# Two-layer hybrid encoder: the MLP's first product with tokens in the rows, its convolution from moved copies, products down in 16, 16 and 12 row tiles

## The chip, the core and the metric

The kernel runs on one core of one Trainium2 chip. The time is device microseconds of one execution; a median is taken over several runs. A profile is one further execution taken by the hardware profiler. Engines: TensorE (PE, its weight loads PEld), VectorE (DVE), ScalarE (ACT), GpSimd (POOL) and SyncE (SP), which only issues DMAs. ScalarE and GpSimd can issue DMAs too, each on a queue of its own. Every engine takes its list of instructions in order and waits at the head of it; 16 DMA engines carry what the queues issue.

## The reference

Two layers on x (256 tokens by 2048), float32. Each layer has a token mixer (attention and a Fourier branch), a cross-attention into 256 memory tokens, and a gated MLP. Every part has an RMS norm before and after it. The change touches the MLP alone:

```python
def conv_ffn(h, w_up, conv_w, conv_b, w_down):
    u = h @ w_up                                  # (256, 2048) @ (2048, 11264)
    up = jnp.pad(u, ((0, 0), (1, 1), (0, 0)))
    u = up[:, :-2] * conv_w[0] + up[:, 1:-1] * conv_w[1] + up[:, 2:] * conv_w[2] + conv_b
    gate, val = u[..., :D_FF], u[..., D_FF:]
    return (jax.nn.gelu(gate, approximate=True) * val) @ w_down   # D_FF = 5632
```

The convolution runs over neighbouring tokens, with three taps and a bias of its own for each of the 11264 channels.

## The kernel before, in words

All products are made of three fp32r products: the operand and the weights are each split in a rounded part (`hi`) and a rest (`lo`), and hi*hi, hi*lo and lo*hi are summed. The activations' parts lie in SBUF (`A_ff`, `G`). Weights stream from HBM: `load` (L110) fetches 128 by 1024 numbers (512 KB, 4 KB in each of 128 partitions) on SP's queue into one of four buffers `w32`; `Unit.split` (L124) makes `whi` with a cast on ScalarE (L133) and `wlo` with a subtraction on VectorE (L134), four buffers each. A unit is two such loads. A load waits for the `wlo` that frees its buffer, a cast for the matmuls that free its `whi`.

**First product, before.** It is channel-major: `ws_chunk` (L163) takes 128 output channels and all 256 tokens. For each of the 16 row tiles, `block` (L148) issues two matmuls, with weights as the stationary operand: `whi` against the 512 columns of both parts of the tokens (L151), `wlo` against the 256 columns of the high part (L152). Channels stand in partitions, tokens along the free dimension. `merge` (L220) adds the two halves of the bank; `conv` (L1189) multiplies by the norm's factor for each token, then uses the taps as one scalar per partition: one activation with scale and bias (L1192) for the middle tap and the bias, and two operations on 255 columns (L1195, L1199) that read the neighbour tokens at an offset of one column. Then come Gelu (L1223), the product of gate and value (L1224), and the split into `G` (L228, L229). This is done 44 times a layer, for a gate chunk and its value chunk. The first 512 columns (`w_up_ko`) are an exception: they are made token-major within the sub-layer's boundary (`Columns`, L305) and turned by eight transposes (L1233).

**Product down, before.** `G` is made in four quarters of 11 row tiles. After each quarter `products` (L371) multiplies it with `w_dn` for four groups of 512 output columns and adds to `y`. `mm_rows` (L296) has the tokens as the stationary operand: for each row tile and each of two token blocks three matmuls of 512 columns (L301 to L303).

**The order of the work.** The Tile scheduler orders each engine's list from the program; the boundaries between sub-layers are ordered by hand. `projected` (L611) and `stream` (L639), which the token mixer uses already, prepare the next unit's weights, then multiply the current one, with a callback between row tiles.

Of the kernel before, what the change touches and what calls it, by code (L numbers as in the profile page):

```python
# [9 lines left out]
F32 = mybir.dt.float32  # L10
# [16 lines left out]
NQ = 4  # L27
QK = DFF // P // NQ
# [8 lines left out]
O_BG, O_CW0, O_CW1, O_CW2, O_CB, NPAR = 112, 144, 232, 320, 408, 496  # L37
# [7 lines left out]
def encoder(ctx: ExitStack, tc: tile.TileContext, t, out):  # L45
# [325 lines left out]
    def products(src, S, nk, begin, finish, last, ahead=(), made=None, mid=None):  # L371

        late = []
        for n in range(4):
            begin(n)
            pss = [psum(f"y{j}") for j in range(2)]
# [5 lines left out]
            for k0 in range(0, nk, 4):  # L385
                m = min(4, nk - k0)
                w = made or unit(src[n][:, k0 * 512 : (k0 + m) * 512], m * 512)
                made = None
                if k0 == 0 and n in ahead:
                    ahead[n]()  # L390
                for k in range(k0, k0 + m):
                    if k >= split_at:
                        late.append((n, pss, k, w, (k - k0) * 512))
                        continue
                    for j in range(2):
                        mm_rows(pss[j], S, k, j, w, (k - k0) * 512, k == 0, k == nk - 1)
            if split_at == nk:
                for j in range(2):
                    finish(j, n, pss[j])
            yield n  # L400
        for j in range(2):
            for i, (n, pss, k, w, col) in enumerate(late):
                mm_rows(pss[j], S, k, j, w, col, k == 0, k == nk - 1)
                if k == nk - 1:
                    finish(j, n, pss[j])
                if j and i + 1 == (mid or len(late) // 2):
                    yield 5
            yield 4 + 2 * j
# [304 lines left out]
    for l in range(L):  # L713
# [448 lines left out]
        cols = Columns(t["w_up_ko"][l], A)  # L1162

        def ahead_apart(y, cols, tags):
# [12 lines left out]
            return {1: lambda: prepare(0), 2: lambda: prepare(1), 3: lambda: sqrt_ahead(y.ss[:, 0, 0:1])}  # L1177

        steps = products(t["w_xo"][l], OX, 4, y.gain, taken, (2,), ahead_apart(y, cols, "B"), w_first)
        for n in range(4):  # L1180
            next(steps)
        ss = boundary(y, steps, par[:, O_FFNPRE : O_FFNPRE + KT], A, cols)
        ut = tmp2("ut"), tmp2("ut")
        ut = [u.rearrange("p a n -> p (a n)") for u in ut]
        for j in range(2):
            nc.scalar.copy(ut[j], cols.ps[j])


        def conv(u, c, name):  # L1189
            nc.vector.tensor_mul(u, u, pre.b)  # L1190
            r = tmp1(name)
            nc.scalar.activation(  # L1192
                r, u, AF.Identity, scale=par[:, O_CW1 + c : O_CW1 + c + 1], bias=par[:, O_CB + c : O_CB + c + 1]
            )
            nc.vector.scalar_tensor_tensor(  # L1195
                out=r[:, 1:T], in0=u[:, 0 : T - 1], scalar=par[:, O_CW0 + c : O_CW0 + c + 1], in1=r[:, 1:T],
                op0=ALU.mult, op1=ALU.add,
            )
            nc.vector.scalar_tensor_tensor(  # L1199
                out=r[:, 0 : T - 1], in0=u[:, 1:T], scalar=par[:, O_CW2 + c : O_CW2 + c + 1], in1=r[:, 0 : T - 1],  # L1200
                op0=ALU.mult, op1=ALU.add,
            )
            return r

        NC = DFF // P
        G = [None] * NQ

        def up(c):

            qt, i = divmod(c, QK)  # L1210
            if i == 0:
                G[qt] = Rows("G") if qt % 2 == 0 else big.tile([P, QK, 2, T], F32R, tag="B", name="G")
            r = []
            for b in range(2):
                if c < 2:
                    u = tmp1("u")
                    nc.scalar.copy(u, firsts[c][:, b])
                else:
                    u = tmp1("u")
# [3 lines left out]
            nc.scalar.activation(r[0], r[0], AF.Gelu_apprx_tanh)  # L1223
            nc.vector.tensor_mul(r[0], r[0], r[1])  # L1224
            split(r[0], G[qt][:, i])

        pre = Pre()
        pre.of_squares(ss)
        third = [ws_chunk(t["w_up"][l, 0], A, KT, name="up")]
        firsts = [ps_sc.tile([P, 2, T], F32, tag="sc", name="ut") for _ in range(2)]  # L1230
        for i in range(4):
            for j in range(2):
                nc.tensor.transpose(  # L1233
                    firsts[i // 2][:, i % 2, j * P : (j + 1) * P], ut[j][:, i * P : (i + 1) * P], ident
                )
        pre.everywhere()
        third.append(ws_chunk(t["w_up"][l, 1], A, KT, name="up"))
        AHEAD = 1
        done = 0
        y = None  # L1240
        for qt in range(NQ):
            until = min(NC, (qt + 1) * QK + (AHEAD if qt + 1 < NQ else 0))
            for c in range(done, until):
                up(c)
            done = until
            if qt == 0:
                y = Out(t["gpost"][l, 2])
            more = qt == NQ - 1 and l + 1 < L

            def first_or_more(j, n, ps, qt=qt):  # L1250
                if qt == 0:
                    nc.scalar.copy(y.at(j, n), ps)
                elif qt < NQ - 1:
                    nc.vector.tensor_add(y.at(j, n), y.at(j, n), ps)
                else:
                    y.take(j, n, ps, True)

            if more:
                A = operand("A_mix")
                cols = Columns(t["w_vu"][l + 1, 0], A)  # L1260

            if more:
                before_last = ahead_apart(y, cols, "CD")
            else:
                before_last = {3: lambda y=y: sqrt_ahead(y.ss[:, 0, 0:1])}

            end = qt == NQ - 1
            steps = products(
                t["w_dn"][l, qt], G[qt], QK, y.gain if end else lambda n: None, first_or_more, 4 if end else QK,
                before_last if end else (), mid=5 if end else None,  # L1270
            )
            for n in range(4):
                next(steps)
            if qt < NQ - 1:
                run(steps)
# [90 lines left out]
def _layout(i):  # L1366
    NC = DFF // P
# [9 lines left out]
    for l in range(L):  # L1377
# [7 lines left out]
        for j, o in enumerate((O_CW0, O_CW1, O_CW2)):  # L1385
            par[l, :, o : o + 2 * NC] = _cols(i["conv_w"][l, j])
# [42 lines left out]
```

## Time and profile before

| | |
|---|---|
| median of 3 runs | 2911.51 us (2911.35 to 2911.95) |
| the profiled execution | 2912.27 us, span 2910.5 us |
| TensorE busy | 2897.6 us of the span |
| VectorE, ScalarE busy | 2053.4 us (71%), 1583.6 us (54%) |
| moved by DMA | 563.09 MB, mean 193 GB/s |
| granted TensorE clock | 0.999 |
| layer 0's MLP between its boundaries | from 744 to 1451 us of the span |
| layer 1's | from 2193.6 to 2896.9 us |

Busy time is the union of an engine's instructions; a matmul's end is modelled, so a busy TensorE says that it had work, not that it ran at its peak. In a group of instructions stand the line, the engine, what is written and read, shapes, the count, then busy time, the mean of one, the idle time just before them and what ended it.

### The profile page before, as it was taken

The page shows a single profiled execution, that of the slowest core. Times are in us where ns is not written, and L with a number is a line of the kernel's source. Part 1 is how long each engine was busy: PE and PEld are TensorE (multiplying, and loading weights), DVE is VectorE, ACT ScalarE, POOL GpSimd, SP SyncE. Part 2 cuts the span into 40 slices and gives each one's busy share as a digit, 9 for nine tenths or more (in the row PEclk, how much of TensorE's full clock was granted, in tenths as well). Part 3 has the DMA queues.
Part 4 walks back from the last instruction along what each step waited for, and adds up shares of the span by engine and source line. Part 5 has one row for each costly group of instructions (what it writes and reads, how often), then busy time and mean ns, then how long its engine had stood idle before and what let it go on. Part 6 is the DMA issues. An engine that isn't in the chain of part 4 may idle for free.

```text
span 2910.5 us, 39133 instructions
## 1 busy us (share of the span) xinstructions
PE 2897.6 (100%) x14476; PEld 2443.7 (84%) x14476; DVE 2053.4 (71%) x2930; ACT 1583.6 (54%) x2479; POOL 34.9 (1%) x60
## 2 busy tenths in 40 slices
PE   9999999999999999999999999999999999999998
PEld 7888888888888888888878888888888888888887
DVE  6668767666875867767776587776678768677676
ACT  6556455555655545545555564445566555455454
POOL 0000000000000000000000000000000000000000
PEclk9999999999999999999999999999999999999999
DMA  8644776765666566565655456677556666666655
GB/s 290 188 148 159 232 235 224 226 187 160 196 184 195 187 188 191 180 200 184 212 174 182 145 163 222 222 236 215 181 159 202 187 193 186 188 190 186 195 185 163
DMA packets 161775, 563.09 MB, mean 193 GB/s; under 512 B 18480, under 2 KB 19504, under 8 KB 161584
## 3 DMA queue, kind: packets, MB, share of 16 engines
q1 hardware_dynamic: 156816, 545.53, 59.5%
q0 software_dynamic: 4480, 14.68, 1.8%
q8 instruction: 113, 1.85, 0.3%
q14 instruction: 78, 0.64, 0.1%
q10 hardware_dynamic: 288, 0.39, 0.0%
HBM read 556.34 MB, written 4.19 MB: 193 GB/s over the span
## 4 chain that ended last, share of the span: by engine, by line
PE 97%; DVE 1%; ACT 1%; DMA 0%; issue 0%; DVEq 0%; ACTq 0%
PE up L151 22%; PE up L152 11%; PE y L302 8%; PE y L303 8%; PE y L301 8%; PE g L301 4%; PE g L303 4%; PE g L302 4%; PE qk L302 3%; PE qk L303 3%; PE qk L301 2%; PE a L301 2%; PE a L303 2%; PE a L302 2%; PE as L302 2%; PE as L301 2%
## 5 line engine op out<-in xcount | busy, mean ns | idle before, releaser
L134 DVE TENSOR_TENSOR wlo<-w,whi 128x1024 fp32r<-128x1024 f32 (+1 forms) x981 | 1179.9, 1205 | 656.4 <-ACT whi L133 649.4
L133 ACT CAST whi<-w 128x1024 fp32r<-128x1024 f32 (+1 forms) x981 | 1015.6, 1037 | 955.6 <-PE y L303 295.4
L151 PE MATMUL up<-A_ff,whi 128*128 128x512 f32 x2688 | 946.3, 397 | 0.0
L152 PE MATMUL up<-A_ff,wlo 128*128 128x256 f32 x2688 | 755.0, 281 | 0.0
L151 PEld LDWEIGHTS up<-A_ff,whi 128*128 128x128 f32 x2688 | 504.9, 188 | 121.9
L152 PEld LDWEIGHTS up<-A_ff,wlo 128*128 128x128 f32 x2688 | 509.0, 189 | 0.4
L301 PE MATMUL y<-whi,G 128*128 128x512 f32 x704 | 274.3, 390 | 0.0
L302 PE MATMUL y<-wlo,G 128*128 128x512 f32 x704 | 274.2, 389 | 0.0
L303 PE MATMUL y<-whi,G 128*128 128x512 f32 x704 | 274.2, 389 | 0.0
L301 PE MATMUL g<-whi,A_mix 128*128 128x512 f32 x512 | 202.3, 395 | 0.0
L302 PE MATMUL g<-wlo,A_mix 128*128 128x512 f32 x512 | 200.8, 392 | 0.0
L303 PE MATMUL g<-whi,A_mix 128*128 128x512 f32 x512 | 200.3, 391 | 0.0
L303 PEld LDWEIGHTS y<-whi,G 128*128 128x128 f32 x704 | 132.2, 188 | 27.5
L301 PEld LDWEIGHTS y<-whi,G 128*128 128x128 f32 x704 | 132.2, 188 | 27.4
L302 PEld LDWEIGHTS y<-wlo,G 128*128 128x128 f32 x704 | 132.2, 188 | 27.2
L303 PE MATMUL qk<-whi,A_mix 128*128 128x512 f32 x320 | 125.6, 392 | 0.0
L302 PE MATMUL qk<-wlo,A_mix 128*128 128x512 f32 x320 | 125.4, 392 | 0.0
L301 PE MATMUL qk<-whi,A_mix 128*128 128x512 f32 x320 | 124.9, 390 | 0.0
L223 ACT COPY t<-up 128x256 f32<-128x256 f32 x168 | 61.7, 367 | 102.8 <-DVE G L229 84.7
L303 PEld LDWEIGHTS g<-whi,A_mix 128*128 128x128 f32 x512 | 96.3, 188 | 19.1
L301 PEld LDWEIGHTS g<-whi,A_mix 128*128 128x128 f32 x512 | 96.3, 188 | 18.4
L302 PEld LDWEIGHTS g<-wlo,A_mix 128*128 128x128 f32 x512 | 96.4, 188 | 17.9
(264 smaller groups left out, 4076.7 us busy)
## 6 DMA issues: line engine op xcount, KB each, us to landing
w<-in_w_up SPq DMA_DIRECT2D x336, 512.0 KB, 4.5
w<-in_w_dn SPq DMA_DIRECT2D x160, 512.0 KB, 4.0
w<-in_w_g SPq DMA_DIRECT2D x128, 512.0 KB, 4.3
w<-in_w_qk SPq DMA_DIRECT2D x80, 512.0 KB, 4.5
w<-in_w_ao SPq DMA_DIRECT2D x64, 512.0 KB, 5.0
w<-in_w_mo SPq DMA_DIRECT2D x64, 512.0 KB, 4.3
w<-in_w_vu SPq DMA_DIRECT2D x47, 512.0 KB, 4.5
w<-in_w_fo SPq DMA_DIRECT2D x32, 512.0 KB, 4.1
```

Source lines behind the costliest of these rows:

```text
L133: nc.scalar.copy(hi[:, :m], w[:, :m])
L134: nc.vector.tensor_sub(lo[:, :m], w[:, :m], hi[:, :m].bitcast(F32))
L151: nc.tensor.matmul(ps, hi, a, start=first, stop=False, skip_group_check=True)
L152: nc.tensor.matmul(ps[:, :T], lo, a[:, 0:T], start=False, stop=last, skip_group_check=True)
L223: nc.scalar.copy(b, ps[:, T : 2 * T])
L301: nc.tensor.matmul(ps, ah, hi, start=first, stop=False)
L302: nc.tensor.matmul(ps, ah, lo, start=False, stop=False)
L303: nc.tensor.matmul(ps, al, hi, start=False, stop=last)
```

## The change

The first product is made token-major throughout. 11264 channels are 22 halves of 512: for column block b (0 to 10) the gate half and the value half. `projected` runs `mm_rows` over the 16 row tiles of a half, for two token blocks (`uv`, "gate" or "val": 128 partitions by 2 token blocks by 512 channels). `finish` evicts both with the norm's factor as scale. Tokens now stand in partitions, so a neighbour token is a neighbour partition. Two copies of the half are made by DMA on ScalarE's queue: `left` (L1240), moved up by one partition, and `right` (L1241), moved down by one; L1242 and L1243 copy the one row each that crosses from one token block to the other. The taps are fetched for each half with `partition_broadcast`, as 128 equal rows of 4 by 512 numbers (1 MB, `cv`, L1226, on SP's queue). VectorE multiplies left, right and own by their taps and sums (L1246, L1250, L1259), six operations on 1024 elements a partition. These are put into a list `due`, and `beside` issues them 7 to 12 row-tile steps after the half was finished. Gelu is one activation of 1024 elements. The gated result is turned by eight transposes a block into `G` (L1272, L1273, 13 and 14 steps after). Products down are made in 16, 16 and 12 row tiles, the first two in the same stream, after the gate halves of blocks 4 and 8; the last by `products`, which takes the first 8 row tiles of two column groups first. Parameters for taps and bias leave `par`; the weights' layout in HBM follows.

```diff
+        def half(i):
+            b, w = divmod(i, 2)
...
+            def finish(j, ps, to):
+                u = places["val" if w else "gate"]
+                nc.scalar.activation(u[:, j], ps, AF.Copy, scale=pre.t[:, j : j + 1])
+                if not j:
+                    return
+                left, right = places["left"], places["right"]
+                nc.scalar.dma_start(left[1:P], u[0 : P - 1])
+                nc.scalar.dma_start(right[0 : P - 1], u[1:P])
+                nc.scalar.dma_start(left[0:1, 1], u[P - 1 : P, 0])
+                nc.scalar.dma_start(right[P - 1 : P, 0], u[0:1, 1])
+
+                def times(v, k):
+                    nc.vector.tensor_mul(v, v, to[:, k : k + 1].to_broadcast([P, 2, 512]))
+
+                def own():
+                    times(u, 1)
+                    nc.vector.tensor_add(u, u, to[:, 3:4].to_broadcast([P, 2, 512]))
...
+                due.extend([(7, lambda: times(left, 0)), (8, lambda: times(right, 2)), (9, own)])
+                due.extend([(n, lambda v=v: nc.vector.tensor_add(u, u, v)) for n, v in ((10, left), (11, right))])
+                due.append((12, activate))
+                if w:
+                    due.extend([(13, lambda: turn(0)), (14, lambda: turn(1))])
+
+            def turn(j):
...
+                for m in range(4):
+                    nc.tensor.transpose(pt[:, m], places["val"][:, j, m * P : (m + 1) * P], ident)
+                hi, lo = [G[q][:, 4 * k : 4 * k + 4, part, j * P : (j + 1) * P] for part in range(2)]
+                nc.scalar.copy(hi, pt)
+                nc.vector.tensor_sub(lo, pt, hi.bitcast(F32))
...
+        def taps(i):
...
+            nc.sync.dma_start(to, t["conv"][l, :, h * 512 : (h + 1) * 512].partition_broadcast(P))
...
+        def up(i):
+            b, w = divmod(i, 2)
+            return projected(t["w_up"][l, b + w * NB], A, "up", half(i), lambda: taps(i))
...
+        for i in range(1, 2 * NB):
+            items += up(i)
+            b = i // 2
+            if i % 2 == 0 and b % DN == 0:
+                q = b // DN - 1
+                for n in range(4):
+                    src = down(q, n)
+                    items += projected([src[:, u * UW : (u + 1) * UW] for u in range(4)], Down(q), "y", sum_down(q, n))
...
-        def conv(u, c, name):
-            nc.vector.tensor_mul(u, u, pre.b)
-            r = tmp1(name)
-            nc.scalar.activation(
-                r, u, AF.Identity, scale=par[:, O_CW1 + c : O_CW1 + c + 1], bias=par[:, O_CB + c : O_CB + c + 1]
-            )
...
-                    ps = third[b] if c == 2 else ws_chunk(t["w_up"][l, 2 * (c - 2) + b], A, KT, name="up")
-                    merge(ps, u)
-                r.append(conv(u, b * NC + c, "cv"))
```

**VectorE, within the first product.** Before, a piece of layer 0 (`t_104` holds the chunk's 256 columns, `w_` numbers are weight buffers):

```order
L134 TENSOR_TENSOR wlo<-w_6935,whi 128x1024 [waits DMAHW7_49,PE_49,Activation_49]
L229 TENSOR_TENSOR G<-t_104,G 128x256 [waits Activation_49]
L224 TENSOR_TENSOR t_104<-up,t_104 128x256 [waits Activation_49]
L1190 TENSOR_TENSOR t_104<-t_104,rb 128x256 [waits DVE_49]
L134 TENSOR_TENSOR wlo<-w_6984,whi 128x1024 [waits DMAHW0_49,PE_49,Activation_49]
L1195 SCALAR_TENSOR_TENSOR t_104<-t_104,par_98 128x255 [waits Activation_49]
L1199 SCALAR_TENSOR_TENSOR t_104<-t_104,par_98 128x255 [waits DVE_49]
```

Now, after a gate half of layer 0 was finished (`uv` holds gate, val, left and right, `cv` the taps; `DMAHW` are the DMAs' semaphores; L135 is what L134 was, and w_8801 and w_8803 are the first unit of the next half, w_8839 and w_8841 the second, w_8877 and w_8879 the third):

```order
L135 TENSOR_TENSOR wlo<-w_8801,whi 128x1024 [waits DMAHW4_49,Activation_49]
L1246 TENSOR_TENSOR uv<-uv,cv 128x1024 [waits DMAHW3_49,DMAHW2_49]
L135 TENSOR_TENSOR wlo<-w_8803,whi 128x1024 [waits DMAHW5_49,PE_49,Activation_49]
L135 TENSOR_TENSOR wlo<-w_8839,whi 128x1024 [waits DMAHW7_49,Activation_49]
L135 TENSOR_TENSOR wlo<-w_8841,whi 128x1024 [waits DMAHW0_49,DVE_49,Activation_49]
L1246 TENSOR_TENSOR uv<-uv,cv 128x1024 [waits DMAHW5_49,DMAHW4_49,DVE_49]
L135 TENSOR_TENSOR wlo<-w_8877,whi 128x1024 [waits DMAHW1_49,Activation_49]
L135 TENSOR_TENSOR wlo<-w_8879,whi 128x1024 [waits DMAHW6_49,Activation_49]
L1246 TENSOR_TENSOR uv<-uv,cv 128x1024
L1250 TENSOR_TENSOR uv<-uv,cv 128x1024 [waits DVE_49]
L135 TENSOR_TENSOR wlo<-w_8919,whi 128x1024 [waits DMAHW7_49,Activation_49]
L1259 TENSOR_TENSOR uv<-uv 128x1024 [waits DVE_49]
```

Before, nothing on VectorE in this stretch but `wlo` waits for a DMA. Now the first L1246 (left) stands between the two `wlo` of one unit and waits for copies, and the second (right) ahead of the third unit's `wlo`.

**ScalarE, where a half is finished.** Before, a piece of layer 0's MLP:

```order
L228 CAST G<-t_104 128x256 [waits DVE_49]
L133 CAST whi<-w_7575 128x1024 [waits DMAHW0_49,PE_49]
L133 CAST whi<-w_7577 128x1024 [waits DMAHW1_49,PE_49,Activation_49]
L133 CAST whi<-w_7611 128x1024 [waits DMAHW2_49,PE_49,Activation_49]
L1252 COPY y<-y_7467 128x512 [waits PE_49]
```

Now, where the gate half of the rows above is finished (L1236 is the eviction):

```order
L1236 ACTIVATE uv<-up_8653,rstd_t 128x512 [waits PE_49]
L1236 ACTIVATE uv<-up_8654,rstd_t 128x512 [waits PE_49]
L1242 DMA uv<-uv 1x16x32 [waits Activation_49]
L1240 DMA uv<-uv 127x1024 [waits Activation_49]
L1241 DMA uv<-uv 127x1024
L1243 DMA uv<-uv 1x16x32 [waits DMAHW5_49]
L134 CAST whi<-w_8803 128x1024
L134 CAST whi<-w_8839 128x1024 [waits DMAHW7_49,PE_49]
```

And where a later value half is finished:

```order
L1236 ACTIVATE uv<-up_9147,rstd_t 128x512 [waits DVE_49]
L1236 ACTIVATE uv<-up_9148,rstd_t 128x512
L1272 CAST G<-gt 128x4x128 [waits PE_49] x2
L1240 DMA uv<-uv 127x1024 [waits DMAHW5_49,Activation_49]
L1241 DMA uv<-uv 127x1024 [waits DMAHW6_49]
L1242 DMA uv<-uv 1x16x32
L1243 DMA uv<-uv 1x16x32 [waits DMAHW7_49,DMAHW5_49]
```

ScalarE issued no DMA in this stretch before; it now issues four after each half. L1242, the row that the left copy needs from the other token block, is issued ahead of both large copies in 14 of a layer's 22 halves, and behind both in 8.

More of the change, by code (lines that the diff above doesn't have):

```diff
@@ L369, in factor, with products @@
             nc.vector.reciprocal(self.r[j], s)
-    def products(src, S, nk, begin, finish, last, ahead=(), made=None, mid=None):
+    def products(src, S, nk, begin, finish, last, ahead=(), made=None, mid=None, first=None, beside=None):
         late = []
-        for n in range(4):
-            begin(n)
-            pss = [psum(f"y{j}") for j in range(2)]
+        order = [(n, k0) for n in range(4) for k0 in range(0, nk, 4)]
+        if first is not None:
+            order.sort(key=lambda u: (u[0] > 1, u[0] < 2 and u[1] >= first, u))
+        pss = {}
+        for n, k0 in order:
+            if n not in pss:
+                begin(n)
+                pss[n] = [psum(f"y{j}") for j in range(2)]
             split_at = nk
@@ L1180, in encoder @@
+            return ahead
+        steps = products(t["w_xo"][l], OX, 4, y.gain, taken, (2,), ahead_apart(y, cols, "B", 1), w_first)
         for n in range(4):
             next(steps)
-        ss = boundary(y, steps, par[:, O_FFNPRE : O_FFNPRE + KT], A, cols)
-        ut = tmp2("ut"), tmp2("ut")
-        ut = [u.rearrange("p a n -> p (a n)") for u in ut]
-        for j in range(2):
-            nc.scalar.copy(ut[j], cols.ps[j])
-        def conv(u, c, name):
-            nc.vector.tensor_mul(u, u, pre.b)
-            r = tmp1(name)
-            nc.scalar.activation(
-                r, u, AF.Identity, scale=par[:, O_CW1 + c : O_CW1 + c + 1], bias=par[:, O_CB + c : O_CB + c + 1]
-            )
[L1195 to L1203, printed above, removed]
@@ L1227, in encoder @@
[L1227 to L1237, printed above, removed]
@@ L1238, in encoder @@
[L1238 to L1275, printed above, removed]
@@ new lines, in encoder, with beside @@
+        G = [None] * 3
+        pre = Pre()
+        due = []
+        places = {}
+        def beside(i=None):
+            now = [f for n, f in due if n == 1]
+            due[:] = [(n - 1, f) for n, f in due if n > 1]
+            for f in now:
+                f()
+        def taps(i):
+            if not places:
+                c, d = [big.tile([P, 8, 512], F32, tag=tag, name=name) for tag, name in (("C", "cv"), ("D", "uv"))]
+                places.update(taps=(c[:, 0:4], c[:, 4:8]), gate=d[:, 0:2], val=d[:, 2:4], left=d[:, 4:6], right=d[:, 6:8])
+                nc.vector.memset(d[:, 4], 0.0)
+                nc.vector.memset(d[:, 7], 0.0)
+            b, w = divmod(i, 2)
+            h = b + w * NB
+            to = places["taps"][w]
+            nc.sync.dma_start(to, t["conv"][l, :, h * 512 : (h + 1) * 512].partition_broadcast(P))
+            return to
@@ new lines, in encoder @@
+        items.append(First())
+        ss = boundary(y, steps, par[:, O_FFNPRE : O_FFNPRE + KT], A, cols, then=items[0].make)
+        pre.of_squares(ss)
+        take = half(0)
+        factors = taps(0)
+        for j in range(2):
+            take(j, cols.ps[j], factors)
+        y = Out(t["gpost"][l, 2])
+        for _ in stream(items, beside):
+            pass
+        more = l + 1 < L
+        if more:
+            A = operand("A_mix")
+            cols = Columns(t["w_vu"][l + 1, 0], A)
+            before_last = ahead_apart(y, cols, "CD", 2)
+        else:
+            before_last = {3: lambda: sqrt_ahead(y.ss[:, 0, 0:1])}
@@ L1276, in encoder @@
+        steps = products(
+            [down(2, n) for n in range(4)], Down(2), 4 * (NB - 2 * DN), y.gain, lambda j, n, ps: y.take(j, n, ps, True), 4,
+            before_last, items[-1].w, mid=5, first=8, beside=beside,
+        )
+        for n in range(4):
+            next(steps)
         if l + 1 < L:
@@ L1397, in _layout @@
         st["w_xo"].append(_rows(i["w_xo"][l]))
[L1398 to L1402 removed]
+        st["w_up"].append(_outer(i["w_up"][l]))
+        st["w_dn"].append(_rows(i["w_down"][l]))
     a["par"] = par
```

120 lines of the change are left out of this document (67 added, 53 removed).

## The prediction

> **What bounds the kernel now.** I read the page first, then the busy time of the MLP's stretch by tile, then the DMA rows, then the groups of VectorE and ScalarE by shape. The page:
>
> ```profile
> span 2910.5 us, 39133 instructions
> PE 2897.6 (100%) x14476; PEld 2443.7 (84%) x14476; DVE 2053.4 (71%) x2930; ACT 1583.6 (54%) x2479; POOL 34.9 (1%) x60
> PE 97%; DVE 1%; ACT 1%; DMA 0%; issue 0%; DVEq 0%; ACTq 0%
> ```
>
> TensorE is idle for 2910.5 - 2897.6 = 12.9 us of the span, and 97% of the chain is its own work. So an edit can win only what it takes off TensorE, and it loses every microsecond for which it makes TensorE wait. Next, the windows over layer 0's MLP between its two boundaries, once for tile `up` (first product; columns: stretch, its length, PE, PEld, DVE, ACT busy with counts, clock, DMA share, GB/s) and once for tile `G` on PE alone (product down):
>
> ```profile
> 744.00:1451.00 707.00, 467.96 (x2657) 407.11 (x2656) 35.36 (x84) 30.85 (x84) 1.00 0.62 192
> 744.00:1451.00 707.00, 238.81 (x1050) 1.00 0.62 192
> ```
>
> 467.96 + 238.81 = 706.8 of the 707 us: the two products fill the stretch. A block of the first product is two matmuls, so 467.96 / 1328.5 = 352 ns; four blocks (one row tile of 128 by 512 columns, 256 tokens) cost 1.409 us. The form that product down uses takes six matmuls for the same work: 6 x 238.81 / 1050 = 1.365 us. I call this a step below.
>
> **The change part by part.**
>
> *Token-major first product.* Each layer has 336 row-tile steps that leave the old form (2688 blocks in all, a quarter of that is 672 steps in two layers). Gain: 672 x (1.409 - 1.365) = 30 us of TensorE. The result must now be turned. The rows for a turn of eight 128x128 pieces and for the engines' work around it:
>
> ```profile
> 744.05 0.87 PE ut L1233 x8
> L134 DVE TENSOR_TENSOR wlo<-w,whi 128x1024 fp32r<-128x1024 f32 x947 | 1156.8, 1224 | 635.8 <-ACT whi L133 628.9
> L1195 DVE SCALAR_TENSOR_TENSOR t<-t,par 128x255 f32<-128x255 f32 x176 | 84.3, 479 | 1.5 <-ACT t L1192 1.3
> L1199 DVE SCALAR_TENSOR_TENSOR t<-t,par 128x255 f32<-128x255 f32 x176 | 85.3, 484 | 6.2
> L1190 DVE TENSOR_TENSOR t<-t,rb 128x256 f32<-128x256 f32 x176 | 74.1, 425 | 5.4
> L224 DVE TENSOR_TENSOR t<-up,t 128x256 f32<-128x256 f32 x168 | 70.7, 421 | 36.1 <-ACT t L223 35.7
> L1224 DVE TENSOR_TENSOR t<-t 128x256 f32<-128x256 f32 x88 | 37.4, 425 | 4.4 <-ACT t L1223 1.0
> L229 DVE TENSOR_TENSOR G<-t,G 128x256 fp32r<-128x256 f32 x88 | 36.8, 419 | 0.0
> L434 DVE TENSOR_TENSOR A_ff<-a,A_ff 128x512 fp32r<-128x512 f32 x16 | 10.9, 689 | 4.5 <-ACT A_ff L430 4.1
> L789 ACT ACTIVATE kug<-u,rstd_t 128x512 f32<-128x512 f32 x8 | 5.3, 682 | 2.0 <-PE u L303 2.0
> L775 ACT CAST O<-rt 128x512 fp32r<-128x512 f32 x16 | 9.4, 588 | 13.3 <-PE rt L772 13.3
> ```
>
> One transpose is 0.87 / 8 = 109 ns. 11 column blocks x 8 x 2 layers = 176 are added and the 16 of `ut` go: 160 x 0.109 = 17.4 us. TensorE's work changes by 17.4 - 30 = -12.5 us.
>
> *VectorE's work.* Removed per layer: 88 x (0.421 + 0.425 + 0.479 + 0.484) + 44 x (0.425 + 0.419) = 196 us. Added per layer: per half (22 of them) six operations on 1024 elements, for which the nearest row is the 1024-element `wlo` at 1.224 us, that is 7.3 us; and per column block one more, and two splits of 512 at 0.689: 22 x 7.3 + 11 x (1.22 + 1.38) = 190 us. No difference in sum. ScalarE has over 40% idle and takes larger, fewer pieces: nothing. Products down in 16, 16 and 12 row tiles have the same number of steps (176 per layer) and fewer sums: nothing.
>
> *The moved copies.* This is the term that decides. Each of 44 halves gets two copies of 127 partitions by 4 KB (520 KB) on ScalarE's queue. Every copy of before has 128 partitions, which sixteen engines share evenly, eight each. 127 is prime: no number of engines between 2 and 16 shares it evenly. The order in the section on the change shows that the builder did cut the single rows of L1242 and L1243 into 16 pieces (1x16x32), and left the 127 rows whole. No row of before shows such a copy, so I bound it from both sides. Shared by 16 engines it lands like a weight load. Left to one engine it takes 127 packet times of that engine one after the other:
>
> ```profile
> w<-in_w_up SPq DMA_DIRECT2D x336, 512.0 KB, 4.5
> out<-X SPq DMA_DIRECT2D x6, 256.0 KB, 2.1
> 5.00:15.00 10.00, 8.65 (x37) 6.37 (x36) 7.68 (x14) 7.19 (x13) 0.00 (x0) 1.00 1.01 381
> 6.00:7.00 1.00, 0.24 (x3) 0.05 (x1) 0.00 (x0) 0.48 (x2) 0.00 (x0) 1.00 1.09 424
> ```
>
> The last two rows are windows of the start, where the share says that all 16 engines are full: 381 and 424 GB/s, so 23.8 and 26.5 GB/s for one engine, and 4096 bytes in 172 or 155 ns. I take 163 ns: a copy is 127 x 0.163 = 20.7 us on one engine against 2.1 to 4.5 us on sixteen. I take one engine, because the count of rows can't be divided. The Trainium skill, "DMA: Bandwidth & Descriptors", section "Why a DMA increments its semaphore by 16 and not by 1", says the same and more: a copy from SP's or ScalarE's queue is spread over the largest number up to 16 that divides the slowest dimension, 127 partitions go to a single engine, and it is always the lowest-numbered one. Nothing in the trace of before shows this either way; by that rule both copies queue on the same engine, which is the case that I sum.
>
> *What waits for them.* The order shows VectorE's list after a half is finished: first the multiplication of the left copy (L1246), then three `wlo` of the next half's weights, then the multiplication of the right copy, then the remaining `wlo`. VectorE takes its list in order, so the `wlo` behind a copy come late, and TensorE needs them. In 14 of a layer's 22 sets TensorE has done 8 of the next half's 16 steps when the second copy is awaited. In 8 sets L1242 stands behind both copies, and its first piece queues behind them; there the left multiplication already waits for all of it, and 10 to 12 steps (11) are left. From a half's last matmul on, for the 14: two evictions at 0.682, two casts at 0.588 and about 1.5 us of the 2.1 us of `out<-X` until data flow, together 4.0; both copies, 2S; one multiplication and one `wlo`, 2.4; then 8 steps, 10.9. Without a wait TensorE would take 16 steps, 21.8. Lost: 2S - 4.5. For the 8: 2S + 6.4 + 11 x 1.365 - 21.8 = 2S - 0.4. The mean is 2S - 3.0.
>
> 2S on the shared engine also holds the packets of the other queue that pass through it meanwhile: three weight loads of 8 packets, as three `wlo` free three buffers, and the new load of taps, 8 packets of 8 KB, which count twice: 40. (254 + 40) x 0.163 = 47.9 us. Lost per set: 44.9 us; 44 sets: 1976 us. The row on SP's own waits says why no more loads than that pass:
>
> ```profile
> SPq L112 <- DVE wlo L134: 1842.9, 770, 20.3
> ```
>
> A load starts when a `wlo` frees its buffer, so loads stop when VectorE stops. The taps' load is new on SP's queue and waits for an earlier half's own product on VectorE; weight loads stand behind it. While VectorE itself waits that adds nothing; it would be seen only if the copies were quick.
>
> **The sum** against the profiled execution: 2912.3 (its span of 2910.5 and 1.8 around it; the median of the runs, 2911.5, is 0.8 lower) - 12.5 + 1976 = 4876, I say 4880 us. Ends: 254 packets of 155 ns with all sets of the better kind, 39.4 - 4.5 = 34.9, give 4435; all eight loads of a half and the taps in between, 334 packets of 172 ns, 57.4 - 0.4 = 57.0, give 5410.
>
> The Trainium skill, "TensorE: Matmul & The Clock Gate", Part 1, says that TensorE's clock falls to half after an idle window and needs about 3.4 us of work to rise. The trace of before, with idle times of a microsecond, grants 1.00 in the windows above and can't show it; 1.7 us more in each of 44 sets would make an estimate of 4955 us.
>
> **Rivals.** (1) One engine per copy, but the two copies on two engines, side by side. For it: nothing says which engine is chosen. Then both land after (127 + 40) x 0.163 = 27.2 us. TensorE has done 2 steps in the 14 sets and 5 in the 8, and goes on at 4.0 + 27.2 + 2.4 = 33.6: lost 33.6 + 14 x 1.365 - 21.8 = 30.9 and 26.8, mean 29.4; 44 x 29.4 = 1294, so 4190 us. Chance 0.06. (2) Shared by all engines after all (unequal shares, 7 rows on the last). The first copy lands 4.5 us after its 4.0, and the `wlo` behind it is there at 8.5 + 2.4 = 10.9, where TensorE stopped at 2.7 us (2 steps) in the 14 and 6.8 (5 steps) in the 8: 8.2 and 4.1, mean 6.7; 44 x 6.7 = 295, so 3200 us. Against it: the undivided 127. Chance 0.06. (3) Not slower: the copies land as quickly as `out<-X`, and the new first product runs faster than product down does. With 2.1 us a set of the 14 still loses 4.0 + 2.1 + 2.4 - 2.7 = 5.8 us, one of the 8 loses 1.7, mean 4.3, in all 190 us. The 672 steps would have to win 190 - 12.5 = 178 us more, 0.26 each, that is 1.10 us per step or 183 ns per matmul, against 227 in the row of `G`. Nothing in the trace runs so fast. Chance 0.03.
>
> **How the numbers follow.** Forecast (one engine for both copies) 0.85, 4880 us. Its own ends hold it about nine times in ten, 0.77; the range reaches down to rival 1: 4180 to 5410 holds about 0.83. About 0.2% is what a measurement of this kernel can tell from no change. All cases but rival 3 are slower: 0.97; of rival 3's 0.03 I give 0.02 to no change and 0.01 to faster.
>
> **What would show it.** Right: L1240 and L1241 near 21 us of transfer each and the second landing some 45 to 50 us after its issue; VectorE's waits led by L1246 on these copies; TensorE's busy share near 60%, with its idle time ahead of `wlo`; DMA share in the MLP far below 0.62; six matmuls per step at 1.37 us when they run. Wrong: copies landing within 5 us, or the right copy landing together with the left; TensorE idle ahead of `whi` instead, with SP waiting at the taps; or a multiplication of 1024 elements far from 1.2 us, which would show that VectorE's pace and not the copies sets the time.

## The result, and the profile after

| | before | changed |
|---|---|---|
| median | 2911.73 us (4 runs, 2911.35 to 2913.66) | 4657.43 us (4 runs, 4652.83 to 4659.26) |
| ratio | | 1.599 [1.596, 1.602] |
| span of the profiled execution | 2910.5 us | 4654.5 us |

The changed kernel is 1746 us slower. The diff moves the lines up by one behind its first hunk: `whi` is now L134, `wlo` L135, `mm_rows` L302 to L304. The page of the changed kernel: busy times, TensorE's busy tenths and its clock by slices, and the chain that ended last.

```profile
span 4654.5 us, 35983 instructions
PE 3092.7 (66%) x13284; PEld 2506.4 (54%) x13284; DVE 2023.5 (43%) x2356; ACT 1465.7 (31%) x2083; POOL 34.8 (1%) x60
PE   9999996333494434944699999964334944349446
PEclk9999998667796767966899999986667976679678
DMA 18%; PE 7%; ACTq 3%; DVE 2%; issue 1%; ACT 1%; DVEq 0%
```

TensorE was busy 2897.6 us before; it now stands still for 4654.5 - 3092.7 = 1562 us, and the slices put this in the two MLPs alone, where 9 becomes 3 or 4. Single slices of 9 between them are products down. The chain, which was 97% TensorE, is led by DMA. Next, its waits (engine and line that waited, what released it; total us, times, longest):

```profile
DVE uv L1246 <- DMA uv<-uv: 1857.4, 72, 46.4
ACT whi L134 <- issue: 1214.1, 46, 33.0
PE up L302 <- ACT whi L134: 795.8, 38, 26.7
PE up L303 <- DVE wlo L135: 502.2, 64, 15.8
SPq L113 <- DVE wlo L135: 3896.5, 934, 47.6
```

VectorE waits 1857 us for the moved copies, a little more than the 1746 us that are lost. SP's loads wait for `wlo`, twice as long as before (1842.9). But TensorE's own waits are split: 502 us stand ahead of `wlo`, as VectorE's wait would make them, and 796 us ahead of `whi`, that is of ScalarE (in the products down it is another 89 and 133 us). ScalarE's 1214 us are put down to "issue". What it issues then stands in the view of tile `uv` (least, median and greatest duration in ns):

```profile
L1240 ACTq DMA_DIRECT2D uv<-uv x44: 612/645/1153, 749.2 to 4540.5; - x44
L1241 ACTq DMA_DIRECT2D uv<-uv x44: 640/8812/13347, 750.4 to 4541.1; - x44
L1243 ACTq DMA_DIRECT2D uv<-uv x44: 546/19677/23287, 759.6 to 4542.6; - x44
```

The first copy is handed over in 0.6 us. The second takes 8.8 us and the edge row behind it 19.7, and ScalarE does nothing else meanwhile. One set (the four copies after one half) in the middle of layer 0's MLP shows both waits. ScalarE (start, us, engine and line, what it waited for):

```profile
2034.20 0.64 ACTq L1240 DMA_DIRECT2D uv<-uv  x1
2034.89 8.51 ACTq L1241 DMA_DIRECT2D uv<-uv  x1
2043.50 19.67 ACTq L1243 DMA_DIRECT2D uv<-uv  x1
2063.20 3.88 ACT L134 CAST whi<-w 128x1024 fp32r<-128x1024 f32 x4 [29.03 <-issue]
...
2094.66 0.65 ACTq L1240 DMA_DIRECT2D uv<-uv  x1
```

VectorE in the same set:

```profile
2057.14 1.22 DVE L1246 TENSOR_TENSOR uv<-uv,cv 128x1024 f32<-128x1024 f32 x1 [23.19 <-DMA uv<-uv]
2064.28 3.50 DVE L135 TENSOR_TENSOR wlo<-w,whi 128x1024 fp32r<-128x1024 f32 x3 [5.92 <-DMA uv<-uv]
2081.92 1.23 DVE L1246 TENSOR_TENSOR uv<-uv,cv 128x1024 f32<-128x1024 f32 x1 [14.14 <-DMA uv<-uv]
```

The left copy is there 22.9 us after its issue (2057.14 - 2034.20) and the right one 24.8 us later: one after the other, 47.7 us in all. The set, from its first large issue to the next set's, takes 60.5 us (to 2094.66) where 16 steps take 21.8. And the matmuls of tile `up` in the three parts of this set, from issue to left product, to right product, to the next issue (length, busy and count, clock, DMA share, GB/s):

```profile
2034.20:2057.14 22.94, 8.14 (x35) 0.72 0.11 42
2057.14:2081.92 24.78, 10.83 (x37) 0.71 0.25 84
2081.92:2094.66 12.74, 10.32 (x35) 0.70 0.66 217
```

A matmul that runs over an edge counts on both sides, and the last part runs some 11 matmuls into the following half. The DMA engines are 11% and 25% busy while everything waits for a DMA: 11% is less than the worth of two engines of the sixteen. In finer slices, all queues together move mostly 21 to 29 GB/s in the first part once the loads in flight have landed, and 26 in the second before the loads go on; the prediction's estimate for one engine was 23.8 to 26.5.

### The profile page after: what moved, and what is told of

Read it like the earlier page. It is cut to its first block, busy times and chain, and to the rows that moved or that the text cites. A ratio compares the mean times of both kernels' runs of the same rounds, so it can differ in the third digit from the quotient of the medians.

```text
span 4654.5 us, 35983 instructions
## 1 busy us (share of the span) xinstructions
PE 3092.7 (66%) x13284; PEld 2506.4 (54%) x13284; DVE 2023.5 (43%) x2356; ACT 1465.7 (31%) x2083; POOL 34.8 (1%) x60
## 3 DMA queue, kind: packets, MB, share of 16 engines
q1 hardware_dynamic: 177744, 591.27, 39.9%
## 5 line engine op out<-in xcount | busy, mean ns | idle before, releaser
L134 ACT CAST whi<-w 128x1024 fp32r<-128x1024 f32 (+1 forms) x965 | 998.3, 1049 | 2826.7 <-issue 1214.1
L135 DVE TENSOR_TENSOR wlo<-w,whi 128x1024 fp32r<-128x1024 f32 (+1 forms) x965 | 1167.7, 1221 | 636.6 <-ACT whi L134 622.0
L302 PE MATMUL up<-whi,A_ff 128*128 128x512 f32 x1344 | 587.2, 438 | 795.8 <-ACT whi L134 795.8
L1246 DVE TENSOR_TENSOR uv<-uv,cv 128x1024 f32<-128x1024 f32 x132 | 161.3, 1222 | 1857.4 <-DMA uv<-uv 1857.4
L303 PE MATMUL up<-wlo,A_ff 128*128 128x512 f32 x1344 | 594.9, 443 | 502.2 <-DVE wlo L135 502.2
L302 PEld LDWEIGHTS up<-whi,A_ff 128*128 128x128 f32 x1344 | 289.1, 216 | 876.5 <-ACT whi L134 811.9
L303 PEld LDWEIGHTS up<-wlo,A_ff 128*128 128x128 f32 x1344 | 289.2, 215 | 596.6 <-DVE wlo L135 533.8
L304 PE MATMUL up<-whi,A_ff 128*128 128x512 f32 x1344 | 578.9, 431 | 0.0
L302 PE MATMUL y<-whi,G 128*128 128x512 f32 x704 | 282.6, 402 | 134.2 <-ACT whi L134 132.7
L304 PEld LDWEIGHTS up<-whi,A_ff 128*128 128x128 f32 x1344 | 289.2, 215 | 61.5
L304 PE MATMUL y<-whi,G 128*128 128x512 f32 x704 | 280.1, 399 | 0.0
L302 PEld LDWEIGHTS y<-whi,G 128*128 128x128 f32 x704 | 136.6, 194 | 166.0 <-ACT whi L134 135.2
L302 PE MATMUL g<-whi,A_mix 128*128 128x512 f32 x512 | 202.2, 395 | 0.0
L304 PE MATMUL g<-whi,A_mix 128*128 128x512 f32 x512 | 200.2, 391 | 0.0
L304 PEld LDWEIGHTS y<-whi,G 128*128 128x128 f32 x704 | 136.4, 194 | 28.4
L304 PE MATMUL qk<-whi,A_mix 128*128 128x512 f32 x320 | 125.3, 392 | 0.0
L302 PE MATMUL qk<-whi,A_mix 128*128 128x512 f32 x320 | 124.9, 390 | 0.0
L1259 DVE TENSOR_TENSOR uv<-uv 128x1024 f32<-128x1024 f32 x88 | 107.3, 1219 | 0.4
```

The costliest lines, as they stand in the source:

```text
L134: nc.scalar.copy(hi[:, :m], w[:, :m])
L135: nc.vector.tensor_sub(lo[:, :m], w[:, :m], hi[:, :m].bitcast(F32))
L302: nc.tensor.matmul(ps, ah, hi, start=first, stop=False)
L303: nc.tensor.matmul(ps, ah, lo, start=False, stop=False)
L304: nc.tensor.matmul(ps, al, hi, start=False, stop=last)
L1246: nc.vector.tensor_mul(v, v, to[:, k : k + 1].to_broadcast([P, 2, 512]))
```

## The experiments

The theory: 127 rows go to one DMA engine as 127 packets of 4 KB, always to the same engine, so that two copies take 48 us one after the other, and VectorE's list, which takes the products of the copies between the `wlo`, passes that on to TensorE. Rivals: the copies share the engines, and something else holds VectorE; or ScalarE's blocked issues, not VectorE's wait, set the time.

**e1: each copy in 112 and 15 rows.** Only the count of rows that one instruction copies changes.

```diff
-                nc.scalar.dma_start(left[1:P], u[0 : P - 1])
-                nc.scalar.dma_start(right[0 : P - 1], u[1:P])
+                nc.scalar.dma_start(left[1 : 112 + 1], u[0:112])
+                nc.scalar.dma_start(left[112 + 1 : P], u[112 : P - 1])
+                nc.scalar.dma_start(right[0:112], u[1 : 112 + 1])
+                nc.scalar.dma_start(right[112 : P - 1], u[112 + 1 : P])
```

> Each copy of 127 rows is cut in two copies, of 112 and of 15 rows; nothing else is changed. Theory A (the 127 rows go to one DMA engine, one packet after the other): 112 rows are seven for each of 16 engines and 15 rows one for each of 15, so a copy lands within 5 us of its issue instead of 23 to 24, ScalarE's issues no longer take 8 and 19 us, and of the 39 us that a set loses now at most 3 to 7 stay: 2950 to 3200 us. Theory B (VectorE's list, with long multiplications and the taps ahead of the weights' subtractions, or ScalarE's six issues, hold TensorE whatever the engines do): no great change, above 4400 us.

Measured: 3129.42 us, ratio to before 1.075 [1.073, 1.077]. 1528 us of the loss are gone with the same bytes. The page's DMA row (KB each, us to landing) and VectorE's wait:

```profile
uv<-uv ACTq DMA_DIRECT2D x88, 448.0 KB, 7.9
DVE uv L1248 <- DMA uv<-uv: 386.5, 47, 12.2
```

**e2: the same with 113 and 14 rows.** As e1, one row moved from the short piece to the long one; 113 is prime too.

```diff
-                nc.scalar.dma_start(left[1 : 112 + 1], u[0:112])
-                nc.scalar.dma_start(left[112 + 1 : P], u[112 : P - 1])
+                nc.scalar.dma_start(left[1 : 113 + 1], u[0:113])
+                nc.scalar.dma_start(left[113 + 1 : P], u[113 : P - 1])
```

(and so for `right`)

> The same cut one row later, 113 and 14 rows. 113 is prime. Theory A with the rule of the largest divisor: 113 rows stay on one engine, 226 packets for the two copies instead of 254; at the 0.18 us a packet that the trace of the change shows, a set gets 5 us shorter: 4440 us, 4350 to 4550. If it were only the size of a copy that mattered (a piece over some limit) or unequal shares were possible, it would come out like the cut at 112.

Measured: 4482.66 us (one run). One row more in the long piece costs 1353 us. So neither the cut nor the number of instructions decides, but the count of rows: 112 is 7 x 16, 113 and 127 are prime. A limit between 112 and 113 rows would fit these two runs as well; the weight loads of 128 rows (from HBM), which land in 4.9 us in e1, speak against it. A count with a divisor in between was not tried. Against the 127 rows, 28 packets a set left the one engine and 174.8 us went, 174.8 / 44 / 28 = 0.142 us a packet.

**e3: the right copy on SP's queue.**

```diff
-                nc.scalar.dma_start(right[0 : P - 1], u[1:P])
+                nc.sync.dma_start(right[0 : P - 1], u[1:P])
```

> The right copy (L1241) is issued on SyncE's queue instead of ScalarE's, the left one stays. Theory A with one fixed engine for every such copy: both still queue on that engine, now from two queues, and land together at about 47 us; since then the left multiplication waits for both, 4650 to 4900 us. If each queue's copy had an engine of its own, both would land after 24 us: about 4000 us.

Measured: 4684.85 us (one run). Another queue brings no other engine. The list of DMA packets in the traces shows it directly. In the changed kernel the 11176 packets of 4 KB on ScalarE's queue (254 a set) start 155 ns apart in the median and never less than 153. Here the left copy's start 311 ns apart, with one of the right copy's, from SP's queue, between each two: two queues take turns on one engine. In e1 the median is 18 ns. The same run speaks on ScalarE; its issues by line in the view of tile `uv`, and two rows of its waits:

```profile
L1241 SPq DMA_DIRECT2D uv<-uv x44: 624/632/738, 748.6 to 4569.1; - x44
L1243 ACTq DMA_DIRECT2D uv<-uv x44: 547/2620/20976, 750.2 to 4569.7; - x44
```

```profile
DVE uv L1246 <- DMA uv<-uv: 1891.1, 44, 44.9
ACT whi L134 <- issue: 469.0, 30, 22.1
```

ScalarE's blocked time falls from 1214 to 469 us and the total does not fall. VectorE still waits 1891 us, now once a set, since both copies share the engine from the start and end together. TensorE's waits have changed sides: 1165 us ahead of `wlo` (502 in the changed kernel), 259 ahead of `whi` (796). Against the rival: ScalarE's block lies beside VectorE's wait.

**e4: no copies.** `left` and `right` are set to zero once a layer, so that the convolution's outer taps are left out, while all operations of VectorE stay.

```diff
-                nc.vector.memset(d[:, 4], 0.0)
-                nc.vector.memset(d[:, 7], 0.0)
+                nc.vector.memset(d[:, 4:8], 0.0)
...
-                nc.scalar.dma_start(left[1:P], u[0 : P - 1])
-                nc.scalar.dma_start(right[0 : P - 1], u[1:P])
-                nc.scalar.dma_start(left[0:1, 1], u[P - 1 : P, 0])
-                nc.scalar.dma_start(right[P - 1 : P, 0], u[0:1, 1])
```

> The four copies of a half are left out; left and right hold zeros that are multiplied and added all the same, so the convolution has its middle tap only. All else of the change stays: the taps' loads, VectorE's operations, the transposes, the stages of product down. Theory A: the copies carry all of the loss: 2890 to 2940 us (2912 less 12.5 by my sum of TensorE's work, plus up to 1 us a half). Theory B, with VectorE's long pieces or the taps' loads costing on their own: above 3000 us.

Measured: 2900.74 us, ratio 0.996 [0.994, 0.997], 11.5 us less than before (2912.21 beside it). The first row is from its page; then the same stretch as in the prediction, for all engines and for tile `up` (PE, PEld, ACT):

```profile
PE 2884.8 (99%) x13284; PEld 2390.1 (82%) x13284; DVE 2029.3 (70%) x2354; ACT 1480.3 (51%) x2083; POOL 34.7 (1%) x60
```

```profile
744.00:1451.00 707.00, 707.00 (x3167) 585.39 (x3166) 502.65 (x458) 333.50 (x366) 1.08 (x2) 1.00 0.71 224
744.00:1451.00 707.00, 460.38 (x2006) 374.60 (x2004) 28.77 (x42) 1.00 0.71 224
```

The copies carry all of the loss: 4657.4 - 2900.7 = 1757 us, 39.9 us a set. TensorE is busy for the whole stretch; the taps' load, the new operations of VectorE and the transposes cost nothing that can be seen.

**e5: all four copies on GpSimd's queue**, with 127 rows as in the change.

```diff
-                nc.scalar.dma_start(left[1:P], u[0 : P - 1])
-                nc.scalar.dma_start(right[0 : P - 1], u[1:P])
+                nc.gpsimd.dma_start(left[1:P], u[0 : P - 1])
+                nc.gpsimd.dma_start(right[0 : P - 1], u[1:P])
```

(and so for the two edge rows)

> All four moved copies are issued on GpSimd's queue instead of ScalarE's, otherwise the changed kernel (one core, 127 rows a copy). ScalarE then issues nothing and can't be held at an issue. If the time is lost because ScalarE stands at its blocked issues (about 28 us a set, 1214 us of waits of whi in the changed kernel), it falls to about 4657 - 1214 = 3440 with copies that still take some 21 us each. If the copies' landing alone sets it, and a queue of GpSimd also gives 127 rows to one fixed engine, it stays at 4600 to 4750. If this queue gives each copy one engine, but another one for the next copy, the copies run side by side: 3900 to 4200. The Trainium skill, DMA: Bandwidth & Descriptors, section Why a DMA increments its semaphore by 16 and not by 1, has an exception by which this queue shares 127 rows over 16 engines; then the copies land in 4 to 10 us and the time is near that of the copies cut into 112 and 15 rows, 3050 to 3200.

Measured: 3082.64 us (one run). The issues of the second copy, now GpSimd's, and then the copies' landing from the page:

```profile
L1241 POOL DMA_DIRECT2D uv<-uv x44: 527/527/530, 748.8 to 3000.7; - x44
```

```profile
uv<-uv POOLq DMA_DIRECT2D x88, 508.0 KB, 8.4
```

The same 127 rows land in 8.4 us from this queue. That agrees with the exception in the Trainium skill, "DMA: Bandwidth & Descriptors", section "Why a DMA increments its semaphore by 16 and not by 1": a software queue on trn2 can share 127 partitions over 16 engines. So it is queue and row count together that leave one engine.

**e6: VectorE's operations later.** On e1: left, right, own product at steps 11, 12, 12 instead of 7, 8, 9; sums at 13, activation at 14, turns at 15 and 16.

```diff
-                due.extend([(7, lambda: times(left, 0)), (8, lambda: times(right, 2)), (9, own)])
+                due.extend([(11, lambda: times(left, 0)), (12, lambda: times(right, 2)), (12, own)])
```

> The copies cut into 112 and 15 rows as in e1_112_15 (3129 us), and VectorE's operations on a half placed later: left product at step 11 instead of 7, right product and own product at 12 instead of 8 and 9, both sums at 13 instead of 10 and 11, activation at 14 instead of 12, turns at 15 and 16 instead of 13 and 14. If what is left of the loss in e1_112_15 is that VectorE reaches the left product before the copies land (387 us of waits in 47 pieces), VectorE now has 4 to 5 steps (5 to 7 us) more of work ahead of it, the waits fall by more than half and the time comes to 2910 to 3000 us. If the copies' share of the DMA engines (with 4 MB of weights and 1 MB of taps a half) or ScalarE's issues set it, it stays at 3060 to 3140.

Measured: 3133.56 us, ratio 1.076 [1.074, 1.078]: no gain, where 2910 to 3000 was expected. The edit did not do what it was made for. VectorE's list shows why (first pieces of a half, e1 with - and e6 with +; the first L1248 is the left product):

```
 L135 TENSOR_TENSOR wlo<-w_6419,whi 128x1024
 L1248 TENSOR_TENSOR uv<-uv,cv 128x1024
+L135 TENSOR_TENSOR wlo<-w_6453,whi 128x1024
 L135 TENSOR_TENSOR wlo<-w_6455,whi 128x1024
-L1248 TENSOR_TENSOR uv<-uv,cv 128x1024
-L135 TENSOR_TENSOR wlo<-w_6457,whi 128x1024
-L1248 TENSOR_TENSOR uv<-uv,cv 128x1024
...
+L1248 TENSOR_TENSOR uv<-uv,cv 128x1024 x2
```

The scheduler left the left product where it was and moved only those behind it, by a place or two. A step in `due` says when an instruction is written, not where it stands.

**e7 and e9: the written order kept.** The same places, with VectorE's list in the MLP's stream fixed to the order of the program; e7 with the copies on GpSimd's queue (e5), e9 with the copies cut on ScalarE's (e6).

```diff
-        for _ in stream(items, beside):
-            pass
+        with tc.manual_schedule(engines={ENG.DVE}):
+            for _ in stream(items, beside):
+                pass
```

> Copies on GpSimd's queue as in e5_pool_queue (3083 us), later places as in e6_late, and in the MLP's stream of units VectorE keeps the order in which the program is written instead of the builder's: the left product now stands behind the two wlo of a half's last unit, which need buffers that come free at the half's eighth step, about 11 us after the copies are issued. If what is left of the loss is that VectorE reaches the left product before the copies land (8 us), its waits for copies all but go and the time falls to 2900 to 2930 us (floor: e4_no_copies, 2901). If it is the copies' traffic, or VectorE with its 90% load of this stretch, the time stays over 2980.

> As e6_late (copies cut into 112 and 15 rows on ScalarE's queue, 3134 us) with VectorE in the written order. If only VectorE's place for the left product is at fault, it comes to the time of e7_pool_hand within 30 us; if ScalarE's issues (up to 8 us in which whi waits at an edge row's issue) cost on their own, it stays 50 us or more above e7_pool_hand.

Measured: e7 3001.04 us, ratio 1.030 [1.028, 1.032]; e9 3011.56 us, 1.035 [1.033, 1.037]. VectorE's wait for the copies in e6, in e7, and TensorE's longest wait in e7:

```profile
DVE uv L1248 <- DMA uv<-uv: 391.4, 44, 13.2
```

```profile
DVE uv L1246 <- DMA uv<-uv: 19.2, 8, 4.7
PE gt L1270 <- DVE uv L1254: 48.0, 22, 2.8
```

The place in the list was worth 122 us (e6 to e9), and the wait for copies is all but gone. e9 is within 11 us of e7, so ScalarE's issues cost little once no copy is left to one engine, although its casts still wait 108 us at them. But neither reaches the 2900 to 2930 expected.

**e8: ScalarE and TensorE in the written order too.**

```diff
-        with tc.manual_schedule(engines={ENG.DVE}):
+        with tc.manual_schedule(engines={ENG.DVE, ENG.Activation, ENG.PE}):
```

> As e7_pool_hand, with ScalarE and TensorE too in the written order in the stream. If the builder's order on ScalarE (casts ahead of evictions) still costs something, a little below e7_pool_hand; if the written order holds evictions behind casts that wait for buffers, above it by up to 2 us a half, 90 us. Both theories of the copies expect it within 3% of e7_pool_hand.

Measured: 3112.09 us, ratio 1.069 [1.067, 1.070], 111 us above e7. TensorE now waits 125.8 us at the transposes for VectorE's last product, 48.0 in e7. Of the three engines the written order helped VectorE; ScalarE and TensorE were changed together, so which of the two loses by it is not shown.

**e10: the transposes at steps 19 and 20** (on e7; but for a layer's last block).

```diff
-                    due.extend([(15, lambda: turn(0)), (16, lambda: turn(1))])
+                    n = 15 if b == NB - 1 else 19
+                    due.extend([(n, lambda: turn(0)), (n + 1, lambda: turn(1))])
```

> As e7_pool_hand (3001 us) with the transposes of a block's gated result at steps 19 and 20 instead of 15 and 16, but for the last block of a layer, since TensorE waits 48 us there for VectorE's last product (22 waits of up to 2.8 us) and 57 us stand before the weight loads of these transposes. If these waits, and TensorE's slower clock behind them, are what is left, the time falls by 50 to 80 us, to 2920 to 2950. If the traffic of the copies (weight loads that take 6.2 us to land instead of 4.9) is what is left, it stays at 2970 to 3000.

Measured: 2983.89 us, ratio 1.023 [1.022, 1.025]. 17 us, not 50 to 80: part of the wait moved to `wlo` (41.1 us of TensorE's, 17.5 in e7). It is the outcome that the expectation gave to the copies' traffic, and e12 tries that.

**e11: VectorE's operations spread further**, on e10.

```diff
-                due.extend([(11, lambda: times(left, 0)), (12, lambda: times(right, 2)), (12, own)])
-                due.extend([(n, lambda v=v: nc.vector.tensor_add(u, u, v)) for n, v in ((13, left), (13, right))])
-                due.append((14, activate))
+                due.extend([(11, lambda: times(left, 0)), (12, lambda: times(right, 2)), (13, own)])
+                due.extend([(n, lambda v=v: nc.vector.tensor_add(u, u, v)) for n, v in ((14, left), (14, right))])
+                due.append((15 if b == NB - 1 else 17, activate))
...
-                    n = 15 if b == NB - 1 else 19
+                    n = 15 if b == NB - 1 else 21
```

> As e10_turns_later, with VectorE's operations spread more evenly between the wlo: the own product and the sums behind the wlo of the next half's first unit, the gating behind the second, the transposes at steps 21 and 22. If VectorE's runs of four operations between two pairs of wlo (4.9 us) still hold wlo back (42 us of waits of TensorE in e7_pool_hand), it comes out 10 to 40 us under e10_turns_later, at 2900 to 2925, level with or below the kernel before (2912); if not, within 10 us of e10_turns_later.

Measured: 3081.77 us, ratio 1.058 [1.056, 1.059]. By my edit the gating comes after the next gate half was evicted, so each value half is multiplied by the next block's gate. The later sums also hold the next copies, which overwrite `left` and `right` (730 us of waits on GpSimd's queue). It says nothing on runs of operations as such.

**e12: e10 without the copies**, as e4 is the change without them.

```diff
-                nc.gpsimd.dma_start(left[1:P], u[0 : P - 1])
-                nc.gpsimd.dma_start(right[0 : P - 1], u[1:P])
-                nc.gpsimd.dma_start(left[0:1, 1], u[P - 1 : P, 0])
-                nc.gpsimd.dma_start(right[P - 1 : P, 0], u[0:1, 1])
```

> e10_turns_later (2984 us) without the four copies: left and right are set to zero once a layer, all of VectorE's operations stay. It leaves the two outer taps of the convolution out. If the 83 us that e10_turns_later stands over e4_no_copies (2901) come from the copies' traffic (1 MB a half beside 5 MB of weights and taps, so that weights land later and casts wait for them), the time falls to 2895 to 2910. If they come from the written order and its longer runs on VectorE, it stays at 2960 to 2985; in between, both have a part.

Measured: 2901.74 us, ratio 0.996 [0.995, 0.998]. Without copies the written order costs nothing (e4 took 2900.74); the last 82 us of e10 are the copies' own. What it changes beside them, ScalarE's casts that wait for weights and the weights' landing, e10 first, then e12:

```profile
ACT whi L134 <- DMA w<-in_w_up: 293.4, 178, 5.5
w<-in_w_up SPq DMA_DIRECT2D x352, 512.0 KB, 6.4
```

```profile
ACT whi L134 <- DMA w<-in_w_up: 48.2, 43, 2.3
w<-in_w_up SPq DMA_DIRECT2D x352, 512.0 KB, 4.8
```

With VectorE's waits for copies down to 20.0 us in e10, the likely path is traffic: the copies pass with the weights, these land 1.6 us later, and the casts wait. Shown is that the copies cost 82 us there; that the weights' delay is the way was not tried by itself. No version that computes all of it was faster than the kernel before.

## Why the prediction was right, and where it was off

**What bounds the kernel.** Held: TensorE's idle time rose by 1562 - 12.9 = 1549 us and its busy time by 195 us, together 1744 of the 1746 us lost.

**TensorE's work, -12.5 us.** e4 puts the whole change but the copies at -11.5 us. By busy time a step took 460.38 x 6 / 2006 = 1.377 us against 1.365. Counted in both traces from each matmul's start to the next, the first product fell from 945.7 to 919.7 us, 26.0 less (30 forecast), and the transposes rose from 1.7 to 15.6 us, 13.9 more (17.4 forecast). So each term held, and not the sum alone.

**VectorE's sum, ScalarE, products down: nothing.** Right for the operations: e4 fills TensorE. Not foreseen on ScalarE: the step counted its evictions and casts and left out its own DMA issues, 28 us a set in which it makes no `whi`. So the sign that I gave for being wrong, TensorE idle ahead of `whi`, came up in 796 us of the waits; SP's waits at the taps (39.4 us) did not. e3 and e1 show that this block is a second face of the same copies: with 745 us of it gone the time is no shorter (e3), and with the copies spread over more engines it falls to 116 us, although ScalarE then issues six of them after each half (e1).

**The moved copies, one engine, both on the same.** Right, by three runs and the packets: 113 rows are nearly as slow as 127 and 112 are not (e2, e1), and SP's queue leads to the same engine (e3). VectorE's 72 waits for copies are those of the two kinds of set: two waits in each of 28 sets, and one, for both copies, in each of the 16 where L1242 stands behind them. Of the rivals, the first (two engines, 4190) fell with the set above, where the copies land one after the other, and with e3, where a second queue brought no second engine. The second (sixteen engines, 3200) is what e1 and e5 make by hand, at 3129 and 3083. The third needed a step of 1.10 us; it has 1.37 to 1.38.

**The packet, 163 ns, and 2S.** 49.4 us were forecast from issue to the second landing (47.9 and 1.5 of start); the set above has 47.7. A packet took 155 ns, not 163: the copies' 254 packets, with those of other queues between them, ran from 2.1 to 46.9 us after the issue, 44.8 us where 47.9 were forecast.

**Lost per set, 44.9 us: the term that was mis-sized.** e4 measures 39.9. I had 8 of the next half's 16 steps left when the second copy is awaited. In the set above TensorE had done some 35 + 37 = 72 of 96 matmuls by then, 12 steps, so 4 are left: 4 x 1.365 = 5.5 us less. By the left product it had already done 35, some six steps, where I had counted two; the three `wlo` behind it gave the other six, as counted. The other sets of this kind have the same 12 steps, but for a layer's first, which has 14; where L1242 stands behind both copies it is some 8 to 10 steps and not 5. Between the first matmuls of two halves, 2033.25 and 2092.07, the set above takes 58.8 us, where the sum gives 21.8 + 47.9 - 4.5 = 65.2. The steps are 5.5 us of this difference. Another 3.2 us is the second landing, 48.7 us after the half's end and not 4.0 + 47.9 = 51.9. Against both works what the main sum left out, the clock. TensorE in the changed kernel, at the first matmuls after a stall (start, duration):

```profile
2021.73 0.80 PE L303 MATMUL up<-wlo,A_ff 128*128 128x512 f32 x1 [14.72 <-DVE wlo L135]
2022.33 0.63 PE L304 MATMUL up<-whi,A_ff 128*128 128x512 f32 x1
2022.76 0.63 PE L302 MATMUL up<-whi,A_ff 128*128 128x512 f32 x1
...
2025.00 0.39 PE L302 MATMUL up<-whi,A_ff 128*128 128x512 f32 x1
2025.23 0.39 PE L303 MATMUL up<-wlo,A_ff 128*128 128x512 f32 x1
```

For some 2.5 us a matmul starts every 0.43 us, then every 0.23. The Trainium skill, "TensorE: Matmul & The Clock Gate", Part 1, says that the clock halves after idling; here the trace agrees. A set of copies has two or three such stalls: TensorE's busy time is 3092.7 - 2884.8 = 208 us more than in e4, 4.7 us a set. But slow matmuls that end while a copy is still awaited cost nothing. In the set above the four steps behind the last stall count: from 2084.34 to 2092.07 they take 7.7 us instead of 5.5, 2.3 more. My estimate from that page of the Trainium skill was 1.7 us a set. Steps, landing and clock, -5.5, -3.2 and +2.3, make the 6.4 us between 65.2 and 58.8. So it is partly luck that the total came so near: a slow clock that the main sum did not hold hid part of the steps' error. The four sets with a product down in them are no better or worse: they take some 148 us, of which its 384 matmuls are 87, and 61 are left.

## What to carry to other kernels

Before a tile is moved by one partition, look at the count of rows in each copy: ScalarE's queue gave 127 or 113 rows to one DMA engine and spread 112, and between 113 and 112 that was worth over 1300 us here. A low DMA share while an engine waits for a DMA is the sign. And a transfer that is put in place of a free offset read needs a place in the list of the engine that consumes it, well behind its landing, and may cost the rest even when its consumer hardly waits for it: the best of the whole versions here took 2984 us, against 2902 for the same kernel without the copies.

## What the runs showed of the hardware that I had not expected

- An engine that issues copies bound for one DMA engine is held at the issue: medians of 8.8 us (L1241) and 19.7 us (L1243) on ScalarE, against 0.5 to 1.1 us for the six issues of e1 and 0.53 us for 127 rows on GpSimd's queue in e5. With the two copies on two queues (e3) the medians are 0.6 and 2.6 us, but the edge row's longest is 21.0 us. After how many packets an issue is held is not shown.
- Two queues whose copies go to one DMA engine take turns there packet by packet: 155 ns between the starts of 4 KB packets from one queue, 311 ns for each of two (changed kernel and e3).
- The same 127 rows land in 8.4 us from GpSimd's queue and in some 23 to 25 us each from ScalarE's.
